# Seven block products instead of eight in three of four chunks of the MLP up projections

## The chip, the cores and the metric

The program runs on one core of a Trainium2 chip. A core has a matrix engine (TensorE, PE in the profile), which multiplies a stationary 128x128 block with a moving operand and adds into one of eight PSUM banks; three engines for elementwise work (VectorE or DVE, ScalarE or ACT, GpSimd or POOL); and a queue (SyncE or SP) that issues most of the transfers from memory. Each engine works through its own instructions in order, and engines wait for one another through semaphores. The metric is the time of one execution on the device, in microseconds (us).

## The reference

Two layers of a decoder trunk, with 528 tokens (16 learned ones ahead of 512), 1024 features wide, all in float32. The part that matters here is the MLP at the end of each layer:

```python
a = rmsnorm(h, mlp_pre_g[l])
f = jnp.square(jax.nn.relu(a @ w_up[l])) @ w_down[l]      # 1024 -> 4096 -> 1024
h = h + rmsnorm(f, mlp_post_g[l])
```

Ahead of it each layer has a mixer: an input projection, sliding-window attention with sinks beside a short gated convolution, and an output projection. The output drops the 16 learned tokens, so layer 1's MLP works on 512 tokens only.

## The kernel before

**Layout.** Features lie on the 128 partitions, tokens along the free axis. `h`, `z`, `a` and `f` are arrays of 8 feature blocks of 128 x 528. A product with a weight matrix goes by weight tiles: one tile gives 128 output features and has 8 blocks (k) of 128x128, one for each block of input features.

**Precision.** Each float32 operand is held as two parts, hi (rounded by a copy on ACT) and lo (the remainder, a subtraction on DVE). `mm3` makes one product of blocks out of three matmuls, hi x hi, hi x lo and lo x hi (L157, L158, L159). All three add into the same PSUM bank.

**Tokens.** In layer 0 a weight tile meets the tokens in two ranges, 272 and 256 columns (`RA`, `RB`). In layer 1's MLP it meets all 512 at once (`full`). A matmul's moving operand is one such range.

**The MLP.** The 4096 inner features go in 4 chunks (`NCH`) of 1024. For each chunk `mlp` makes 8 up tiles (a to f, evacuated by `f_evac`: relu on DVE out of PSUM, square on ACT, split into hi on ACT and lo on DVE) and then 8 down tiles (f to z, `z_evac`: a copy in the first chunk, later an addition on DVE). The norm's scale isn't applied to `a` but later; so `a` is h times a gain. In chunk 1 the first 5 up tiles are made together with the norm at the end of the mixer.

**Weights.** The list `blocks` holds all weight tiles of the program in order of use. `prep` loads the next one (512 KB, issued by SP, into one of two buffers `wraw`), and `cast` splits it in two halves of 128x512 (L98 on ACT, L99 on DVE). `tile_done`, called when a tile's products are written down, lets `refill` prepare as many more as keep 7 tiles ready (`CAP`; 5 in the mixer, `PCAP`).

**Order.** A scheduler that knows the dependences fixes each engine's order of instructions when the program is built; it may move an instruction ahead of others of its engine. The waits themselves are then what the chip makes of it.

Of the kernel before, what the change touches and what calls it, by code (L numbers as in the profile page):

```python
# [13 lines left out]
P = 128  # L14
# [3 lines left out]
L = 528  # L18
# [8 lines left out]
BOTH = ()  # L27
# [10 lines left out]
def trunk_kernel(ctx, tc, xT, gains, sinkb, sinkm, rope, masks, maskm, ident_in, w_in, w_out, w_up, w_down, outT):  # L38
# [57 lines left out]
    def cast(i, raw, hi, lo, pool):
        ks = slice(4 * i, 4 * i + 4)
        ACT.activation(hi[:, ks, :], raw[:, ks, :], AF.Copy)  # L98
        (POOL if i in pool else DVE).tensor_tensor(lo[:, ks, :], raw[:, ks, :], hi[:, ks, :].bitcast(F32), ALU.subtract)  # L99

    def prep(pool=(), beside=None):

        if len(prepared) == len(blocks):
            return
        kind, l, sub = blocks[len(prepared)]
        raw = wp.tile([P, KT, P], F32, tag="wraw", name="wraw", bufs=2)
        hi = wp.tile([P, KT, P], F32R, tag="w", name="whi", bufs=2 * CAP)
        lo = wp.tile([P, KT, P], F32R, tag="w", name="wlo", bufs=2 * CAP)
        dma = nc.sync.dma_start
        if beside:  # L110

            for i in range(2):
                ks = slice(4 * i, 4 * i + 4)
                dma(raw[:, ks, :], w_in[l].rearrange("(k p) m -> p k m", p=P)[:, ks, sub:sub + P])
                beside[2 * i]()
                cast(i, raw, hi, lo, pool)
                beside[2 * i + 1]()
            prepared.append((hi, lo))
            return
        if kind == "in":  # L120
            last_load[:] = [dma(raw, w_in[l].rearrange("(k p) m -> p k m", p=P)[:, :, sub:sub + P])]
        elif kind == "out":
            col = slice(P * sub, P * sub + P)
            for g in range(2):
                dma(raw[g * 64:(g + 1) * 64, 0:4, :],
                    w_out[l, g * 256:(g + 1) * 256, col].rearrange("(j p) m -> p j m", p=64))
            dma(raw[:, 4:8, :], w_out[l, 512:1024, col].rearrange("(k p) m -> p k m", p=P))
        elif kind == "up":
            dma(raw, w_up[l].rearrange("(k p) m -> p k m", p=P)[:, :, P * sub:P * sub + P])
# [22 lines left out]
    def tile_done(pool=(), most=9):  # L152
        done[0] += 1
        refill(pool, most)

    def mm3(ps, whi, wlo, ahi, alo, first, last):
        PE.matmul(ps, whi, ahi, start=first, stop=False)  # L157
        PE.matmul(ps, whi, alo, start=False, stop=False)  # L158
        PE.matmul(ps, wlo, ahi, start=False, stop=last)  # L159
# [222 lines left out]
    def first_tiles(act, pB, rA, rB, nxt):  # L382
# [602 lines left out]
```

## Time and profile before

| | us |
|---|---|
| median of 3 runs | 1174.88 (1174.23 to 1175.05) |
| the profiled execution | 1173.51 |
| its span in the trace | 1171.4 |
| PE busy, of the span | 1122.2 |
| DVE busy | 683.1 |
| ACT busy | 550.8 |
| one chunk of layer 0's MLP (up, then down) | 46.88 + 46.88 |
| one chunk of layer 1's MLP (up, then down) | 44.60 + 44.60 |

The span is what the trace covers; the time has some 2 us more around it. In the rows that follow L157 is line 157 of the kernel, and `ps<-a_hi,whi` says what is written and what is read. A group's line gives its count, then busy time in us and the mean duration of one in ns, then how long its engine had been idle before it and what ended that. A line of waits gives the sum in us, how often, and the longest. A line of the timeline gives start, length, engine, line, operation, tiles and shape, and in brackets the idle time ahead of it. Matmuls are pipelined: one starts long before the one ahead of it has ended.

### The profile page before, as it was taken

Reading aid. Unit: us, or ns where it says so; the run is one execution under the profiler, and the core shown is the slowest. Engines: PE = TensorE matmul, PEld = TensorE weight load, DVE = VectorE, ACT = ScalarE, POOL = GpSimd, SP = SyncE. Lnnn points to the kernel's source line nnn. Section 1 sums busy time; section 2 is a strip of 40 time slices with the busy share of each in tenths; the row PEclk is TensorE's granted clock in tenths of the full one; section 3 lists DMA queues with packets and bytes.
Section 4 is the critical chain, followed back from the end, with each engine's and each line's share of the span. In section 5 each row is a group of like instructions: output and inputs, shape, how many; then the busy total and the mean of one; then the engine's idle time right before and its main releaser. Section 6 shows DMA issues by size and latency. Waiting matters only on the chain. (4 is left out here: it accounts for less than half of the span.)

```text
span 1171.4 us, 19765 instructions
## 1 busy us (share of the span) xinstructions
PE 1122.2 (96%) x7778; PEld 1050.6 (90%) x7778; DVE 683.1 (58%) x1613; ACT 550.8 (47%) x1286; POOL 19.0 (2%) x54
## 2 busy tenths in 40 slices
PE   8999899899999999999989997998999999999995
PEld 7999899899999999999979997898888888888895
DVE  7988877762353354355589778777623433433435
ACT  7565776563342242244366557665523412422432
POOL 3000000000000000000000000000000000000001
PEclk9999999899999999999989999998999999999998
DMA  7242122243333333333131321222433333333302
GB/s 229 65 127 73 50 60 84 61 133 88 95 91 87 94 90 89 94 91 90 34 103 50 110 73 36 73 76 70 135 99 90 91 101 97 90 91 104 93 1 72
DMA packets 195069, 101.92 MB, mean 87 GB/s; under 512 B 4832, under 2 KB 194928, under 8 KB 194976
## 3 DMA queue, kind: packets, MB, share of 16 engines
q1 hardware_dynamic: 194368, 100.14, 29.7%
q8 instruction: 61, 1.00, 0.4%
q10 hardware_dynamic: 432, 0.32, 0.1%
q14 instruction: 32, 0.26, 0.1%
q0 software_dynamic: 176, 0.21, 0.1%
HBM read 97.88 MB, written 2.10 MB: 85 GB/s over the span
## 5 line engine op out<-in xcount | busy, mean ns | idle before, releaser
L157 PE MATMUL ps<-a_hi,whi 128*128 128x256 f32 (+3 forms) x1384 | 426.5, 309 | 6.8 <-ACT a_hi L294 5.8
L158 PE MATMUL ps<-a_lo,whi 128*128 128x256 f32 (+3 forms) x1384 | 423.2, 306 | 4.9 <-DVE a_lo L299 4.2
L159 PE MATMUL ps<-a_hi,wlo 128*128 128x256 f32 (+3 forms) x1384 | 421.5, 305 | 0.1
L98 ACT ACTIVATE whi<-wraw 128x512 fp32r<-128x512 f32 x360 | 207.1, 623 | 368.9 <-PE ps L158 337.4
L157 PE MATMUL ps<-f_hi,whi 128*128 128x256 f32 (+2 forms) x1072 | 326.4, 306 | 0.0
L158 PE MATMUL ps<-f_lo,whi 128*128 128x256 f32 (+2 forms) x1072 | 326.1, 305 | 0.0
L159 PE MATMUL ps<-f_hi,wlo 128*128 128x256 f32 (+2 forms) x1072 | 325.2, 305 | 0.0
L99 DVE TENSOR_TENSOR wlo<-wraw,whi 128x512 fp32r<-128x512 f32 x360 | 233.9, 687 | 106.4 <-ACT whi L98 100.1
L157 PEld LDWEIGHTS ps<-a_hi,whi 128*128 128x128 f32 x1384 | 265.6, 192 | 19.9 <-ACT a_hi L294 7.7
L158 PEld LDWEIGHTS ps<-a_lo,whi 128*128 128x128 f32 x1384 | 265.7, 192 | 18.2 <-DVE a_lo L299 6.6
L159 PEld LDWEIGHTS ps<-a_hi,wlo 128*128 128x128 f32 x1384 | 266.5, 193 | 10.1 <-DVE wlo L99 0.4
L158 PEld LDWEIGHTS ps<-f_lo,whi 128*128 128x128 f32 x1072 | 201.4, 188 | 9.8
L159 PEld LDWEIGHTS ps<-f_hi,wlo 128*128 128x128 f32 x1072 | 201.8, 189 | 9.1
L157 PEld LDWEIGHTS ps<-f_hi,whi 128*128 128x128 f32 x1072 | 200.9, 188 | 9.7
L469 DVE TENSOR_TENSOR z<-z,ps 128x272 f32<-128x272 f32 (+2 forms) x78 | 38.1, 488 | 148.0 <-PE ps L159 148.0
L241 DVE TENSOR_TENSOR acc<-acc,t 128x256 f32<-128x256 f32 (+1 forms) x133 | 56.4, 425 | 17.2 <-ACT t L240 15.3
L868 DVE TENSOR_SCALAR t<-ps 128x272 f32<-128x272 f32 (+1 forms) x74 | 31.5, 430 | 54.9 <-PE ps L159 54.8
L868 DVE TENSOR_SCALAR u<-ps 128x512 f32<-128x512 f32 x27 | 18.7, 692 | 69.8 <-PE ps L159 69.8
L869 ACT ACTIVATE t<-t 128x272 f32<-128x272 f32 (+1 forms) x74 | 30.4, 415 | 46.3 <-DVE t L868 46.3
L245 DVE TENSOR_TENSOR f_lo<-t,f_hi 128x272 fp32r<-128x272 f32 (+1 forms) x74 | 31.5, 432 | 25.8 <-ACT f_hi L244 25.8
L240 ACT ACTIVATE t<-z 128x256 f32<-128x256 f32 (+1 forms) x55 | 22.0, 414 | 51.3 <-DVE z L469 37.5
L294 ACT ACTIVATE a_hi<-h,gt 128x256 fp32r<-128x256 f32 (+1 forms) x48 | 24.4, 509 | 26.9 <-DVE h L288 26.7
(130 smaller groups left out, 839.6 us busy)
## 6 DMA issues: line engine op xcount, KB each, us to landing
wraw<-in_w_up SPq DMA_DIRECT2D x64, 512.0 KB
wraw<-in_w_down SPq DMA_DIRECT2D x64, 512.0 KB
wraw<-in_w_in SPq DMA_DIRECT2D x34, 512.0 KB
wraw<-in_w_out SPq DMA_DIRECT2D x32, 128.0 KB
wraw<-in_w_out SPq DMA_DIRECT2D x16, 256.0 KB
outT<-h SPq DMA_DIRECT2D x14, 128.0 KB
h<-in_xT SPq DMA_DIRECT2D x4, 272.0 KB
wraw<-in_w_in SPq DMA_DIRECT2D x4, 256.0 KB
```

What stands on the lines that cost most here:

```text
L98: ACT.activation(hi[:, ks, :], raw[:, ks, :], AF.Copy)
L99: (POOL if i in pool else DVE).tensor_tensor(lo[:, ks, :], raw[:, ks, :], hi[:, ks, :].bitcast(F32), ALU.subtract)
L157: PE.matmul(ps, whi, ahi, start=first, stop=False)
L158: PE.matmul(ps, whi, alo, start=False, stop=False)
L159: PE.matmul(ps, wlo, ahi, start=False, stop=last)
L240: ACT.activation(sq, src, AF.Square)
L241: return (eng or DVE).tensor_tensor(acc, acc, sq, ALU.add)
L245: DVE.tensor_tensor(lo, src, hi.bitcast(F32), ALU.subtract)
L294: self.act = ACT.activation(a_hi[:, k, t0:t1], hk, AF.Copy, scale=g)
L469: DVE.tensor_tensor(zz, zz, ps, ALU.add)
L868: DVE.tensor_scalar(f, ps, 0.0, None, ALU.max)
L869: ACT.activation(f, f, AF.Square)
```

## The change

In chunks 2, 3 and 4 of both layers' up projections, two weight tiles (outputs m and m+1) are taken together with two halves of the tokens (264 and 264 in layer 0, 256 and 256 in layer 1: N0 and N1) and two halves of the input features (k 0 to 3 and 4 to 7). That makes a product of 2x2 blocks with 2x2 blocks, which is done in Winograd's form of Strassen's scheme: seven block products of 4 k each instead of eight.

- *Weights.* A11 and A12 are tile m's two feature halves, A21 and A22 those of tile m+1. `prep_pair` loads the four halves and makes S1 = A21 + A22, S2 = A11 - S1, S3 = A21 - A11 and S4 = A12 + S2, four additions of 128x512 on DVE. All seven left operands are split into hi and lo: seven casts a pair, where two tiles took four.
- *Activations.* B11, B21 are the feature halves over N0, B12, B22 over N1. `fast_sums` makes T1 = B12 - B11 (which overwrites B12 in `a`), T2 = T1 - B22, T3 = B12 - B22 and T4 = B21 + T2, once per layer, after the first four down tiles of chunk 1. They lie in the attention's key and value arrays and in a new array `tx`; `clear_pad` zeroes the keys' padding again ahead of layer 1.
- *Products.* `fast_pair` runs A11 B11 (bank b1), S2 T2 (b6), S3 T3 (b7), S1 T1 (b5), and then adds A12 B21 onto b1, A22 T4 onto b7 and S4 B22 onto b5, each after the bank has been read. Six reads of PSUM on DVE and one on ACT combine them into the four blocks of f; relu, square and split follow.
- *Bookkeeping.* All weights are now loaded in halves of 256 KB, into five half buffers. Prefetch is counted in halves: a product of the new kind counts one, a normal tile two, and 14 are kept ready. The scratch space for transfers issued by software is cut to 1024 bytes.

The core of the diff:

```diff
+    def half():
+        return wp.tile([P, 4, P], F32, tag="wraw", name="wraw", bufs=5)
+    def cast(raw, hi, lo):
+        ACT.activation(hi, raw, AF.Copy)
+        DVE.tensor_tensor(lo, raw, hi.bitcast(F32), ALU.subtract)
+    def prep_pair(l, m, n):
+        if n == 0:
+            for name, k, mm in (("A11", 0, m), ("A21", 0, m + 1), ("A22", 4, m + 1), ("A12", 4, m)):
+                pair[name] = half()
+                nc.sync.dma_start(pair[name], w_up[l].rearrange("(k p) m -> p k m", p=P)[:, k:k + 4, P * mm:P * mm + P])
...
+        f = wp.tile([P, KT, P], F32R, tag="w", name="wf", bufs=2 * CAP)
+        if n == 1:
+            pair["S1"], pair["S2"] = (utile()[:, :512].rearrange("p (k m) -> p k m", k=4) for _ in range(2))
+            DVE.tensor_tensor(pair["S1"], pair["A21"], pair["A22"], ALU.add)
+            DVE.tensor_tensor(pair["S2"], pair["A11"], pair["S1"], ALU.subtract)
+        if n == 2:
+            pair["S3"] = pair["A21"]
+            DVE.tensor_tensor(pair["S3"], pair["A21"], pair["A11"], ALU.subtract)
+        if n == 6:
+            pair["S4"] = pair["S2"]
+            DVE.tensor_tensor(pair["S4"], pair["A12"], pair["S2"], ALU.add)
+        cast(pair[("A11", "S2", "S3", "S1", "A12", "A22", "S4")[n]], f[:, 0:4, :], f[:, 4:8, :])
...
-        while len(prepared) - done[0] < cap[0] and len(prepared) < len(blocks) and most:
-            prep(pool)
+        while len(prepared) < len(blocks) and taken[0] + size(len(prepared)) <= 2 * cap[0] and most:
+            prep()
...
+    def fast_sums(l, k):
...
+        DVE.tensor_tensor(d, h[:, k, N1], h[:, k, N0], ALU.subtract)
+        ACT.activation(x, h[:, k + 4, N1], AF.Copy, scale=g2)
+        hi, lo = parts("T1")
+        ACT.activation(hi, d, AF.Copy, scale=g1)
+        DVE.scalar_tensor_tensor(t2, d, g1, x, ALU.mult, ALU.subtract)
+        DVE.scalar_tensor_tensor(lo, d, g1, hi.bitcast(F32), ALU.mult, ALU.subtract)
+        DVE.scalar_tensor_tensor(t3, h[:, k, N1], g1, x, ALU.mult, ALU.subtract)
+        split(*parts("T2"), t2)
+        DVE.scalar_tensor_tensor(t4, h[:, k + 4, N0], g2, t2, ALU.mult, ALU.add)
+        split(*parts("T3"), t3)
+        split(*parts("T4"), t4)
+    def fast_pair(l, m):
...
+        b1, b6, b7, b5 = (bank()[:, :n] for _ in range(4))
+        def product(ps, name, onto=False):
+            whi, wlo = prepared[wtile()]
+            hi, lo = T[name]
+            for k in range(4):
+                mm3(ps, whi[:, k, :], wlo[:, k, :], hi[:, k, :], lo[:, k, :], not onto and k == 0, k == 3, onto)
+            tile_done()
+        def plus(a, ps):
+            t = tmp(n)
+            DVE.tensor_tensor(t, a, ps, ALU.add)
+            return t
+        def out(x, m, N):
+            ACT.activation(x, x, AF.Relu)
+            ACT.activation(x, x, AF.Square)
+            split(f_hi[:, m, N], f_lo[:, m, N], x)
+        product(b1, "B11")
+        p1 = tmp(n)
+        ACT.activation(p1, b1, AF.Copy)
+        product(b6, "T2")
+        u2 = plus(p1, b6)
+        product(b7, "T3")
+        u3 = plus(u2, b7)
+        product(b5, "T1")
+        out(plus(u3, b5), m + 1, N1)
+        product(b1, "B21", True)
+        x = tmp(n)
+        DVE.tensor_scalar(x, b1, 0.0, None, ALU.max)
+        ACT.activation(x, x, AF.Square)
+        split(f_hi[:, m, N0], f_lo[:, m, N0], x)
+        product(b7, "T4", True)
+        out(plus(u2, b7), m + 1, N0)
+        product(b5, "B22", True)
+        out(plus(u2, b5), m, N1)
...
         for c in range(NCH):
-            for m in range(NA if c == 0 else 0, 8):
-                one(lambda r: f_evac(m, r), act_a)
+            if c == 0:
+                for m in range(NA, 8):
+                    one(lambda r: f_evac(m, r), act_a)
+            else:
+                for m in range(0, 8, 2):
+                    fast_pair(l, m)
             last = c == NCH - 1
             if last:
                 new_acc("h")
             for m in range(2 if last else 8):
                 one(lambda r: z_evac(m, r, c > 0, last, (l, G_MPOST)), act_f)
+                if c == 0 and m < 4:
+                    fast_sums(l, m)
```

The scheduler places the new instructions, so the diff doesn't show their order. On VectorE, at the start of an up projection of layer 0, evacuations (relu out of PSUM, L868, and the low part, L245) and casts (L99) followed each other like this before:

```order
L868 TENSOR_SCALAR t<-ps 128x272
L245 TENSOR_TENSOR f_lo<-t,f_hi 128x272
L868 TENSOR_SCALAR t<-ps 128x256
L99 TENSOR_TENSOR wlo<-wraw,whi 128x512 x2
L245 TENSOR_TENSOR f_lo<-t,f_hi 128x256
```

Now the first pair of chunk 3 begins as follows. L955 is an addition out of PSUM, L974 the maximum with zero out of PSUM, L281 the low part of f, L109 a weight cast, and L131, L124 are the weight sums S4 and S1.

```order
L955 TENSOR_TENSOR t<-t,ps 128x264
L109 TENSOR_TENSOR wf<-u,wf 128x512
L955 TENSOR_TENSOR t<-t,ps 128x264
L131 TENSOR_TENSOR u<-wraw,u 128x512
L109 TENSOR_TENSOR wf<-wraw,wf 128x512
L955 TENSOR_TENSOR t<-t,ps 128x264
L109 TENSOR_TENSOR wf<-u,wf 128x512
L974 TENSOR_SCALAR t<-ps 128x264
L109 TENSOR_TENSOR wf<-wraw,wf 128x512
L124 TENSOR_TENSOR u<-wraw 128x512
L281 TENSOR_TENSOR f_lo<-t,f_hi 128x264
L955 TENSOR_TENSOR t<-t,ps 128x264
```

Casts and sums of later weights now stand between the reads of PSUM that free a bank, up to three between two of them.

On TensorE, where an up projection of layer 0 ends and the down projection begins, the rows before were these, the last matmuls on `a` and then the first on `f`:

```order
L158 MATMUL ps<-a_lo,whi 128x256
L159 MATMUL ps<-a_hi,wlo 128x256
L157 MATMUL ps<-f_hi,whi 128x272
L158 MATMUL ps<-f_lo,whi 128x272
L159 MATMUL ps<-f_hi,wlo 128x272
```

Now (L193 to L195 are `mm3`) the first six matmuls of the down projection, its k 0 and 1, stand ahead of the pair's last two products, A22 T4 and S4 B22; here the end of A12 B21 and the first of the six:

```order
L194 MATMUL ps<-a_lo,wf 128x264
L195 MATMUL ps<-a_hi,wf 128x264
L193 MATMUL ps<-f_hi,whi 128x272
L194 MATMUL ps<-f_lo,whi 128x272
L195 MATMUL ps<-f_hi,wlo 128x272
```

After the last product follow, in layer 0, 12 matmuls of 272 and 18 of 256 columns and then 18 of a second tile, before the first that reads feature blocks 6 and 7 of f; in layer 1, 12 matmuls of 512 columns.

More of the change, by code (lines that the diff above doesn't have):

```diff
@@ L26 @@
 LAST_ON_POOL = (3, 6)
-BOTH = ()
 EPS = 1e-6
@@ L94, in trunk_kernel @@
     used = [0]
[L96 to L101, printed above, removed]
+    done = [0]
+    taken = [0]
+    cap = [CAP]
+    def half():
[3 more added lines that the diff above has]
+        DVE.tensor_tensor(lo, raw, hi.bitcast(F32), ALU.subtract)
@@ L103, in prep @@
+    def prep(beside=None):
         if len(prepared) == len(blocks):
             return
+        taken[0] += size(len(prepared))
         kind, l, sub = blocks[len(prepared)]
-        raw = wp.tile([P, KT, P], F32, tag="wraw", name="wraw", bufs=2)
+        if kind == "upx":
+            return prep_pair(l, *sub)
         hi = wp.tile([P, KT, P], F32R, tag="w", name="whi", bufs=2 * CAP)
         lo = wp.tile([P, KT, P], F32R, tag="w", name="wlo", bufs=2 * CAP)
-        dma = nc.sync.dma_start
-        if beside:
+        raws = []
+        for i in range(2):
+            raw = half()
+            raws.append(raw)
+            ks = slice(4 * i, 4 * i + 4)
+            dma = nc.sync.dma_start
+            if kind == "out":
+                col = slice(P * sub, P * sub + P)
+                if i == 0:
+                    for g in range(2):
+                        dma(raw[g * 64:(g + 1) * 64], w_out[l, g * 256:(g + 1) * 256, col].rearrange("(j p) m -> p j m", p=64))
+                else:
+                    dma(raw, w_out[l, 512:1024, col].rearrange("(k p) m -> p k m", p=P))
+            elif kind == "down":
+                c, m = sub
+                dma(raw, w_down[l, c * 1024:(c + 1) * 1024, P * m:P * m + P].rearrange("(k p) m -> p k m", p=P)[:, ks, :])
+            else:
+                src, off = (w_in, sub) if kind == "in" else (w_up, P * sub)
+                last_load[:] = [dma(raw, src[l].rearrange("(k p) m -> p k m", p=P)[:, ks, off:off + P])]
+            if beside:
+                beside[2 * i]()
+                cast(raw, hi[:, ks, :], lo[:, ks, :])
+                beside[2 * i + 1]()
+        if not beside:
@@ L133, in prep @@
-        for i in range(2):
-            cast(i, raw, hi, lo, pool)
+                cast(raws[i], hi[:, ks, :], lo[:, ks, :])
         prepared.append((hi, lo))
@@ new lines, in fast_sums @@
+    def fast_sums(l, k):
+        N0, N1, T = fast(l)
+        n = N0.stop - N0.start
+        g1, g2 = (gt[:, l, G_MPRE + i:G_MPRE + i + 1] for i in (k, k + 4))
+        d, x, t2, t3, t4 = (tmp(n) for _ in range(5))
+        parts = lambda name: [t[:, k, :] for t in T[name]]
+        DVE.tensor_tensor(d, h[:, k, N1], h[:, k, N0], ALU.subtract)
[9 more added lines that the diff above has]
+        split(*parts("T4"), t4)
```

82 lines of the change are left out of this document (43 added, 39 removed).

## The prediction

> **What bounds the kernel now.** I read the page's first table, then busy time by stage, then single rows. The first says that TensorE (PE) is the engine to look at:
>
> ```profile
> span 1171.4 us, 19765 instructions
> PE 1122.2 (96%) x7778; PEld 1050.6 (90%) x7778; DVE 683.1 (58%) x1613; ACT 550.8 (47%) x1286; POOL 19.0 (2%) x54
> ```
>
> A mean over the span says nothing on the stages that change, so next come the stretches (length; busy time of PE, weight loads, VectorE, ScalarE, GpSimd; clock; DMA share; GB/s). The first two lines are the up and the down projection of chunk 2 in layer 0, the next two those of chunk 2 in layer 1:
>
> ```profile
> 306.15:353.03 46.88, 46.88 (x387) 46.88 (x385) 23.27 (x46) 21.49 (x47) 0.00 (x0) 1.00 0.31 91
> 353.03:399.91 46.88, 46.88 (x387) 46.88 (x385) 17.64 (x33) 9.94 (x18) 0.00 (x0) 1.00 0.32 91
> 889.40:934.00 44.60, 44.60 (x193) 36.05 (x192) 19.40 (x31) 17.81 (x32) 0.00 (x0) 1.00 0.32 95
> 934.00:978.60 44.60, 44.60 (x193) 36.06 (x192) 15.82 (x26) 10.39 (x19) 0.00 (x0) 1.00 0.33 95
> ```
>
> PE is busy in every microsecond, at a granted clock of 1.00. VectorE (DVE) and ScalarE (ACT) work half the time or less, and what they wait for is PE:
>
> ```profile
> ACT whi L98 <- PE ps L158: 337.4, 107, 5.8
> DVE z L469 <- PE ps L159: 148.0, 74, 5.3
> DVE u L868 <- PE ps L159: 69.8, 25, 3.8
> SPq L129 <- DVE wlo L99: 307.0, 56, 16.8
> ```
>
> The last line says that up-weight loads wait for a free buffer, 307 us in all: loads run ahead. So in these stages a matmul less is time less, until another engine fills up.
>
> **What a matmul costs.** Matmuls overlap, so a row's duration (about 0.29 us) is no price; the distance between the evacuations of finished tiles is. Layer 0:
>
> ```profile
> 403.12 0.44 DVE L868 TENSOR_SCALAR t<-ps 128x272 f32<-128x272 f32 x1 [1.17 <-PE ps L159]
> 405.97 0.42 DVE L868 TENSOR_SCALAR t<-ps 128x256 f32<-128x256 f32 x1 [1.00 <-PE ps L159]
> 408.98 0.44 DVE L868 TENSOR_SCALAR t<-ps 128x272 f32<-128x272 f32 x1 [0.76 <-PE ps L159]
> ```
>
> From 403.12 to 405.97 lie 24 matmuls of 256 columns: 0.1188 us each. From 403.12 to 408.98 lie 48, half of 256 and half of 272: 0.1221 on average, which is also my price for 264 columns. Layer 1, 24 matmuls of 512 between two rows, 0.2321 each:
>
> ```profile
> 894.97 0.69 DVE L868 TENSOR_SCALAR u<-ps 128x512 f32<-128x512 f32 x1 [3.85 <-PE ps L159]
> 900.54 0.69 DVE L868 TENSOR_SCALAR u<-ps 128x512 f32<-128x512 f32 x1 [2.74 <-PE ps L159]
> ```
>
> **The change on PE.** A pair of weight tiles took 2 tiles x 8 k x 3 matmuls over all tokens. Now it takes 7 products x 4 k x 3 = 84 matmuls over half of them. Per chunk of four pairs that is 336.
> - Layer 0: 46.88 becomes 336 x 0.1221 = 41.0; 5.86 less, in three chunks 17.6.
> - Layer 1: 44.60 becomes 336 x 0.1188 = 39.9; 4.7 less, in three chunks 14.1. Here one eighth (5.6) isn't reached, because two matmuls of 256 cost 0.2376 and one of 512 0.2321. In return weight loads, 81% busy in this stage now, go to what layer 0 shows, 100%; there they hold at 0.1188 a step, so I charge no more.
>
> Together 31.7 us. PE gets 1008 matmuls of 264 and 1008 of 256 columns for 1152 of 272 and 256 and 576 of 512. The order of the changed kernel shows all of them, with nothing done twice: it does what it says.
>
> **The change on DVE and ACT.** This is where it could be lost. Back-to-back prices first (the next instruction's start counts, not the duration, 0.69 for the cast):
>
> ```profile
> L99 DVE TENSOR_TENSOR wlo<-wraw,whi 128x512 fp32r<-128x512 f32 x360 | 233.9, 687 | 106.4 <-ACT whi L98 100.1 <-PE ps L158 0.2
> L98 ACT ACTIVATE whi<-wraw 128x512 fp32r<-128x512 f32 x360 | 207.1, 623 | 368.9 <-PE ps L158 337.4 <-DMA wraw<-in_w_in 15.7 <-DMA wraw<-in_w_down 11.7
> 46.27 1.29 DVE L99 TENSOR_TENSOR wlo<-wraw,whi 128x512 fp32r<-128x512 f32 x2
> 47.48 0.42 DVE L524 TENSOR_TENSOR t<-t 128x256 f32<-128x256 f32 x1
> 27.04 0.43 DVE L540 TENSOR_TENSOR u<-ps,rt 128x272 f32<-128x272 f32 x1
> 27.39 0.47 DVE L350 SCALAR_TENSOR_TENSOR a_lo<-h,gt,a_hi 128x256 fp32r<-128x256 f32 x1
> 727.66 1.14 ACT L98 ACTIVATE whi<-wraw 128x512 fp32r<-128x512 f32 x2
> 728.71 0.51 ACT L611 ACTIVATE S<-S,ng 128x256 f32<-128x256 f32 x1
> 715.14 1.61 ACT L759 ACTIVATE f_hi<-t 128x256 fp32r<-128x256 f32 x4
> ```
>
> A DVE cast or a weight sum of 512 costs 1.21 / 2 = 0.605; an addition out of PSUM 0.35, the low part of a split likewise. On ACT a cast is 0.525, an evacuation step 1.61 / 4 = 0.40.
>
> Per chunk DVE gets 24 evacuations out of PSUM, 16 low parts, 28 casts and 5 weight sums during the up stage (the order puts the other 11 into the down stage): 40 x 0.35 + 33 x 0.605 = 34 us of 41. ACT: 28 x 0.525 + 48 x 0.40 = 34 us of 41. Both rise from half busy to 83%. Uneven, though: prefetch runs 14 products ahead, so the first two pairs of a chunk prepare products (7 casts and 4 sums a pair) and the last two prepare down tiles. In the first pair of chunk 3 the order has 11 weight rows, 6 evacuations and 3 low parts: 11 x 0.605 + 9 x 0.35 = 9.8 us, against 84 x 0.1221 = 10.26 on PE. That is 96%, and 98% in layer 1 (84 x 0.1188 = 10.0). The densest stretch of the present trace with an unbroken PE is this, DVE 26.19 of 29, 90%:
>
> ```profile
> 29.00:58.00 29.00, 29.00 (x242) 28.95 (x241) 26.19 (x67) 17.82 (x47) 0.87 (x3) 1.00 0.25 66
> ```
>
> At that 90% the pair's rows take 10.9 us, 0.6 to 0.9 longer than PE. So DVE falls behind by some 1.5 us in the first two pairs and catches up in the other two. What does a delay do? Nothing else waits on DVE there but weights, which lie 14 products ahead, and PSUM banks. Eight banks hold two pairs, so a new pair takes free ones. Three products of a pair accumulate onto a bank that must have been read first: onto b1 three products after its first use, onto b7 and b5 two products after, 24 matmuls or 2.93 us. The addition needs 0.44, so about 2.5 us of lag are covered. I charge 0.4 us a chunk for single late rows, 2.4 in all; what the lag costs without that cover stands under the rivals.
>
> The handover from up to down is the other place. The last product's result runs through an addition, relu, square and a split. Today's four steps took from 309.36 to 311.20 = 1.84 us; a fifth makes 2.3:
>
> ```profile
> 309.36 0.44 DVE L868 TENSOR_SCALAR t<-ps 128x272 f32<-128x272 f32 x1 [1.17 <-PE ps L159]
> 310.76 0.44 DVE L245 TENSOR_TENSOR f_lo<-t,f_hi 128x272 fp32r<-128x272 f32 x1 [0.96 <-ACT f_hi L244]
> ```
>
> In layer 0 the order leaves 48 matmuls (5.9 us) before f's feature blocks 6 and 7 are read: covered. In layer 1 it leaves 12 of 512 columns, 2.8 us, with other rows queued ahead: I charge 0.5 us in each of three chunks, 1.5.
>
> The half sums of the activations, 32 rows on DVE and 20 on ACT, come once per layer in chunk 1's down stage, before the weights for chunk 2's first products. They cost 32 x 0.42 = 13.4 and 20 x 0.40 = 8 us, and these stages have room (DVE 11.18 of 46.85 and 11.63 of 44.60) even with 11 weight sums (6.7) on top of as many casts as now:
>
> ```profile
> 259.30:306.15 46.85, 46.85 (x387) 46.85 (x385) 11.18 (x18) 15.03 (x33) 0.00 (x0) 1.00 0.32 91
> 844.80:889.40 44.60, 44.60 (x193) 36.06 (x192) 11.63 (x18) 13.77 (x26) 0.00 (x0) 1.00 0.35 101
> ```
>
> PE's cover there is the whole down stage; uncovered, 21 us a layer.
>
> Weight loads become halves of 256 KB: the same bytes, twice the issues on SP. In the MLP SP has room. In the mixers the small rope transfers share SP's queue and may leave earlier or later; five half buffers instead of two whole ones free a little earlier. I take 0, with bounds of 2 us either way (ACT's waits for w_in loads, 15.7 above, are all there is to win). The padding memsets on GpSimd run while it is idle: 0.
>
> Sum: -31.7 + 2.4 + 1.5 = -27.8. The profiled execution took 1173.51 (span 1171.4), so 1145.7; the median is 1.4 higher, 1174.88, which gives **1147**.
>
> **A rule against it.** After idle moments close together this trace shows the clock halved:
>
> ```profile
> 206.49 0.39 PE L157 MATMUL ps<-a_hi,whi 128*128 128x272 f32 x1 [0.77 <-ACT a_hi L294]
> 208.00 0.39 PE L158 MATMUL ps<-a_lo,whi 128*128 128x272 f32 x1 [1.11 <-DVE a_lo L299]
> 211.76 1.22 PE L196 MATMUL ps<-acc,ones 128*128 128x256 f32 x2 [1.27 <-DVE acc L241]
> ...
> 213.00 0.43 PE L158 MATMUL ps<-a_lo,whi 128*128 128x272 f32 x1
> 213.23 0.43 PE L159 MATMUL ps<-a_hi,wlo 128*128 128x272 f32 x1
> ...
> 216.84 0.28 PE L157 MATMUL ps<-a_hi,whi 128*128 128x272 f32 x1
> 216.96 0.29 PE L158 MATMUL ps<-a_lo,whi 128*128 128x272 f32 x1
> ...
> 740.99 0.50 PE L163 MATMUL ps<-p,vv 128*128 128x512 f32 x1 [1.63 <-ACT p L244]
> 741.33 0.28 PE L157 MATMUL ps<-f_hi,whi 128*128 128x256 f32 x1
> 741.45 0.28 PE L158 MATMUL ps<-f_lo,whi 128*128 128x256 f32 x1
> ```
>
> From 213.00 to 216.84 stand 17 matmuls at 0.226, where 272 columns cost 0.125 at full clock (405.97 to 408.98, 24 of them): 1.7 us lost. After the single gap of 1.63 us at 740.99 steps stayed at 0.12. The Trainium skill ("TensorE: Matmul & The Clock Gate", section "A second HAM failure mode: psum-queue depth-cycling") says that a PE which cycles through PSUM banks and idles a little between groups lets its clock swing between half and full. By that rule gaps at every pair would cost 1.7 us each on top, 24 x 1.7 = 41 us more (an estimate from the row), and the change would be slower; by the row at 740.99 a lone gap every 10 us costs its own length. My sum goes by the row, and has hardly a gap.
>
> **Rivals.**
> - *Nothing is lost* (0.10): all cover holds, mixers gain a little. 31.7 off: 1143. For it: lags stay under 2.5 us by the sum. Against: 96% of DVE is more than any stretch here shows.
> - *DVE sets the pace* in the first two pairs (0.15). At full durations (0.69 and 0.44) the first pair's rows come to 11 x 0.69 + 9 x 0.44 = 11.5 us, 1.3 more than PE; 12 such pairs 15.6, with handovers of 1 us in six chunks 21.6: 31.7 - 21.6 leaves 10.1, 1165. For it: casts hand over between ACT and DVE, both over 80% busy. Against: back-to-back rows at 0.605.
> - *PE stops at the re-used bank* (0.08, slower). If the addition that reads b5 stands behind casts that wait for ACT or for a load, PE waits in front of the pair's last product, and every later product is late by as much, which nothing makes up. It decides from 31.7 / 24 = 1.32 us a pair; at 1.5 it is 36 us, 1174.9 - 31.7 + 36 = 1179. It needs a lag of 4 us, some seven weight rows. This is where the clock rule above would come in. Against: between two evacuations the order has at most three such rows.
> - Between the last two, gain and loss even out (0.05): 1175.
>
> **How the numbers follow.** The forecast, 1147, has 0.62 and its own range, 1143 to 1155: no loss at one end; at the other 1.2 us of lag in six chunks, 1 us in three handovers and 2 us in the mixers, 12.2 together. About 0.2% (2.3 us) is what a measurement here can tell from no change. Faster: 0.62 + 0.10 + 0.15 = 0.87; same 0.05; slower 0.08. The range goes from 1141 (full gain and 2 us in the mixers) to 1165, where the pace case ends; outside lie the slower case, the even one and a little of the others.
>
> **What would show it.** Right: up stages of 41.0 to 42 us (layer 0) and 39.9 to 41 (layer 1) with PE busy throughout, DVE and ACT near 34 us there; down stages unchanged; 8066 matmuls; chunk 1's down stage still 46.9 and 44.6. Wrong: idle PE ahead of matmuls on b5 or b7, released by DVE additions; rows of 0.23 us per matmul in up stages; mixers that changed by more than 2 us.

## The result and the profile after

The changed kernel takes 1140.62 us (median of 4 runs, 1140.13 to 1141.1); the kernel before takes 1174.97 (4 runs beside them). The ratio is 0.9709, 95% interval 0.9692 to 0.9726: 34.3 us less, where 27.8 were forecast. The time lies 0.4 us below the lower end of the predicted range. Two later measurements of the same changed kernel gave 0.972 (0.9707 to 0.9733) and 0.9713 (0.9697 to 0.9729), 33.4 and 34.2 us.

The first table of the page after:

```profile
span 1138.8 us, 21453 instructions
PE 1088.9 (96%) x8066; PEld 1042.9 (92%) x8066; DVE 822.3 (72%) x1941; ACT 641.2 (56%) x1542; POOL 20.2 (2%) x56
```

PE's busy time falls by 33.3 us, the span by 32.6; DVE's rises by 139. The stretches of the kernel after (length; busy time of PE, weight loads, DVE, ACT, GpSimd; clock; DMA share; GB/s): chunk 1's down stage and chunk 2's up and down stages in layer 0, then the same three in layer 1.

```profile
258.82:305.59 46.77, 46.77 (x386) 46.77 (x385) 29.31 (x60) 22.02 (x53) 0.00 (x0) 1.00 0.22 63
305.59:347.24 41.65, 41.65 (x345) 41.65 (x343) 34.03 (x70) 31.90 (x73) 0.00 (x0) 1.00 0.45 130
347.24:393.27 46.03, 46.03 (x381) 46.03 (x379) 24.64 (x45) 10.74 (x21) 0.00 (x0) 1.00 0.23 67
...
826.42:871.01 44.59, 44.59 (x193) 36.07 (x192) 21.86 (x37) 14.97 (x28) 0.00 (x0) 1.00 0.23 65
871.01:912.17 41.16, 41.16 (x344) 40.89 (x342) 34.11 (x71) 32.03 (x74) 0.00 (x0) 1.00 0.47 135
912.17:955.53 43.36, 43.36 (x188) 35.03 (x187) 22.00 (x36) 10.41 (x20) 0.00 (x0) 1.00 0.24 68
```

PE is busy in every microsecond of them. Each up stage here holds six matmuls of the down projection that the scheduler drew forward, so the comparable number is a whole chunk: 41.65 + 46.03 = 87.68 in layer 0 against 93.76 before, 41.16 + 43.36 = 84.52 in layer 1 against 89.20. That is 6.08 and 4.68 us a chunk, three times each: 32.3 of the 32.6 by which the span shrank. Chunk 1's down stage, with the half sums of the activations in it, is unchanged (46.77, 44.59). The rest of the program gives 0.3 in all: the stretch to chunk 2 is 0.56 shorter, layer 1 up to its chunk 2 is 0.62 longer (301.94 after, 301.32 before), and 0.4 lies behind the six chunks. The stretch from layer 1's start to its chunk 2, before:

```profile
587.87:889.19 301.32, 281.20 (x1941) 261.69 (x1940) 214.18 (x566) 171.75 (x432) 2.49 (x10) 0.95 0.29 82
```

And after:

```profile
569.07:871.01 301.94, 280.50 (x1941) 261.44 (x1940) 231.61 (x608) 178.06 (x451) 2.48 (x10) 0.95 0.27 77
```

Does DVE fall behind, as forecast? Yes. The timeline of the kernel after in chunk 2's first pair, three rows of PE and then four of DVE:

```profile
311.31 0.28 PE L195 MATMUL ps<-a_hi,wf 128*128 128x264 f32 x1
...
314.25 0.28 PE L195 MATMUL ps<-tx,wf 128*128 128x264 f32 x1
314.37 0.29 PE L193 MATMUL ps<-a_hi,wf 128*128 128x264 f32 x1
...
312.33 0.42 DVE L955 TENSOR_TENSOR t<-t,ps 128x264 f32<-128x264 f32 x1
...
314.81 0.69 DVE L124 TENSOR_TENSOR u<-wraw 128x512 f32<-128x512 f32 x1 [1.11 <-DMA wraw<-in_w_up]
315.41 0.69 DVE L109 TENSOR_TENSOR wf<-wraw,wf 128x512 fp32r<-128x512 f32 x1
316.02 0.42 DVE L955 TENSOR_TENSOR t<-t,ps 128x264 f32<-128x264 f32 x1
```

S1 T1 ends on b5 at about 311.6; it is read at 312.33, 0.7 us late. The next product on b5 starts at 314.37, 1.6 us after that read is done. A22 T4 ends at 314.5 and is read at 316.02, 1.5 us late, behind a weight sum, which had waited 1.11 us for its load, and a cast. Nothing on PE waits for either. Over all 24 pairs the reads that free b7 and b5 are at most 1.4 us late.

### The profile page after: what moved, and what is told of

Its sections match the earlier page's. It is cut to its first block, busy times and chain, and to the rows that moved or that the text cites. A ratio compares the mean times of both kernels' runs of the same rounds, so it can differ in the third digit from the quotient of the medians.

```text
span 1138.8 us, 21453 instructions
## 1 busy us (share of the span) xinstructions
PE 1088.9 (96%) x8066; PEld 1042.9 (92%) x8066; DVE 822.3 (72%) x1941; ACT 641.2 (56%) x1542; POOL 20.2 (2%) x56
## 4 chain that ended last, share of the span: by engine, by line
PE 87%; DVE 7%; ACT 3%; issue 1%; DMA 1%; SPq 0%; DVEq 0%; POOL 0%; ACTq 0%
PE ps L195 28%; PE ps L193 28%; PE ps L194 27%; PE ps L199 2%; DVE wlo L109 1%; PE ps L232 1%; ACT S L647 1%; DMA h<-in_xT 1%; DVE acc L277 1%; PE ps L693 1%; DVE p L281 1%; DVE a_lo L335 0%; DVE S L658 0%; DVE z L706 0%; DVE h L324 0%
## 5 line engine op out<-in xcount | busy, mean ns | idle before, releaser
L195 PE MATMUL ps<-f_hi,wlo 128*128 128x256 f32 (+2 forms) x1072 | 325.4, 305 | 0.0
L193 PE MATMUL ps<-f_hi,whi 128*128 128x256 f32 (+2 forms) x1072 | 323.7, 306 | 0.0
L193 PE MATMUL ps<-a_hi,whi 128*128 128x256 f32 (+3 forms) x808 | 242.5, 302 | 7.2 <-ACT a_hi L330 6.2
L194 PE MATMUL ps<-a_lo,whi 128*128 128x256 f32 (+3 forms) x808 | 238.5, 295 | 4.6 <-DVE a_lo L335 4.1
L195 PE MATMUL ps<-a_hi,wlo 128*128 128x256 f32 (+3 forms) x808 | 237.1, 294 | 0.3 <-DVE wlo L109 0.3
L195 PEld LDWEIGHTS ps<-f_hi,wlo 128*128 128x128 f32 x1072 | 201.9, 189 | 9.2
L193 PEld LDWEIGHTS ps<-f_hi,whi 128*128 128x128 f32 x1072 | 200.1, 188 | 9.3
L109 DVE TENSOR_TENSOR wlo<-wraw,whi 128x512 fp32r<-128x512 f32 x264 | 173.1, 686 | 44.0 <-ACT whi L108 21.3
L193 PEld LDWEIGHTS ps<-a_hi,whi 128*128 128x128 f32 x808 | 157.7, 196 | 11.9 <-ACT a_hi L330 8.2
L194 PEld LDWEIGHTS ps<-a_lo,whi 128*128 128x128 f32 x808 | 158.2, 196 | 9.3 <-DVE a_lo L335 6.5
L195 PEld LDWEIGHTS ps<-a_hi,wlo 128*128 128x128 f32 x808 | 158.5, 196 | 1.8 <-DVE wlo L109 0.5
L194 PE MATMUL ps<-a_lo,wf 128*128 128x264 f32 (+1 forms) x384 | 108.0, 283 | 0.0
L193 PE MATMUL ps<-a_hi,wf 128*128 128x264 f32 (+1 forms) x384 | 107.8, 283 | 0.0
L195 PE MATMUL ps<-a_hi,wf 128*128 128x264 f32 (+1 forms) x384 | 107.1, 283 | 0.0
L109 DVE TENSOR_TENSOR wf<-wraw,wf 128x512 fp32r<-128x512 f32 x96 | 65.5, 686 | 10.9 <-ACT wf L108 9.8
L194 PEld LDWEIGHTS ps<-a_lo,wf 128*128 128x128 f32 x384 | 72.2, 188 | 0.1
```

Source lines behind the costliest of these rows:

```text
L109: DVE.tensor_tensor(lo, raw, hi.bitcast(F32), ALU.subtract)
L193: PE.matmul(ps, whi, ahi, start=first, stop=False, skip_group_check=onto)
L194: PE.matmul(ps, whi, alo, start=False, stop=False, skip_group_check=onto)
L195: PE.matmul(ps, wlo, ahi, start=False, stop=last, skip_group_check=onto)
```

## The experiments

The kernel before was run again beside each group: 1173.26 us beside the first four kernels, 1173.56 beside the two lighter loads, the scratch and the first repeat, 1174.07 beside x_cover2, the heavier loads and the two edits together, 1173.35 and 1174.36 beside the buffer runs. Ratios are to these.

**Bookkeeping alone** (x_halves): loads in halves, five half buffers, the new counting of prefetch; every up projection as before.

```diff
-            if c:
+            if False:
                 blocks += [("upx", l, (8 * c + 2 * m, n)) for m in range(4) for n in range(7)]
...
-            if c == 0:
-                for m in range(NA, 8):
+            if True:
+                for m in range(NA if c == 0 else 0, 8):
...
-                if c == 0 and m < 4:
-                    fast_sums(l, m)
```

> All up projections as before; only the bookkeeping of the change stays (weights loaded in halves of 256 KB into five buffers, prefetch counted in halves, smaller scratch space). Theory (the gain is matmuls alone): 1175, within 1.5 of before. Rival (loads in halves speed up the start or the mixers, and that is the gain beyond the forecast): 1172 or less.

1170.44 us, ratio 0.9978 (0.9966 to 0.9989): 2.6 us less, just outside the bound of 2 that the prediction had set, so the rival of this run holds.

**The seven products in layer 0 alone** (x_layer0).

```diff
-            if c:
+            if c and l == 0:
                 blocks += [("upx", l, (8 * c + 2 * m, n)) for m in range(4) for n in range(7)]
...
-            if c == 0:
-                for m in range(NA, 8):
+            if c == 0 or l != 0:
+                for m in range(NA if c == 0 else 0, 8):
...
-                if c == 0 and m < 4:
+                if c == 0 and m < 4 and l == 0:
```

> Seven products in layer 0 only. Theory: three chunks of 6.1 us as the trace of the changed kernel shows, so 1175 - 18.2 = 1156.8, and layer 1 is the rest, 14 to 16. Rival (the two layers help each other, for example through the mixer between them): more than 2 us away from that.

1155.61 us, ratio 0.9848 (0.9825 to 0.9871). Chunk 2 of layer 0, up and down stage, in x_halves:

```profile
307.03:353.80 46.77, 46.77 (x386) 46.77 (x385) 23.27 (x46) 21.50 (x47) 0.00 (x0) 1.00 0.31 91
353.80:400.58 46.78, 46.78 (x387) 46.78 (x385) 17.62 (x33) 9.96 (x18) 0.00 (x0) 1.00 0.32 91
```

The same in x_layer0:

```profile
307.67:349.31 41.64, 41.64 (x344) 41.64 (x343) 34.10 (x70) 31.95 (x73) 0.00 (x0) 1.00 0.45 131
349.31:395.34 46.03, 46.03 (x380) 46.03 (x379) 24.64 (x45) 10.74 (x21) 0.00 (x0) 1.00 0.23 66
```

With the bookkeeping the same on both sides the seven products take 93.55 to 87.67, 5.88 us a chunk; the prediction's step has 5.86.

**How much cover the re-used banks need** (x_cover2, x_cover1, x_cover0): the seven products held to one order, with two, one or no product between the use of b7 and b5 and their re-use. The first is the control: the change's own order, but fixed.

```diff
+            with ExitStack() as es:
+                if last_mm:
+                    es.enter_context(tc.issue_after(last_mm[0].ins))
+                for k in range(4):
...
         product(b5, "T1")
         out(plus(u3, b5), m + 1, N1)
-        product(b1, "B21", True)
...
         product(b7, "T4", True)
         out(plus(u2, b7), m + 1, N0)
         product(b5, "B22", True)
         out(plus(u2, b5), m, N1)
+        product(b1, "B21", True)
...
```

That is x_cover1 (x_cover2 has the first hunk alone: each product's matmuls are issued after those of the product ahead). x_cover0 also runs T4 ahead of T1, so that T4 follows T3 on b7, and B22 follows T1 on b5.

> The changed kernel with the seven products of a pair held to one order, B11 T2 T3 T1 B21 T4 B22 (two products between the use of b7 or b5 and its re-use), which is the control for the two fixed orders with less between. If the loss of the order with one product between comes from the re-used banks, this one takes 1140 to 1141. If it comes from holding the order at all, which keeps TensorE from taking other matmuls in between, it takes 1142 to 1143 as well.

> The products of a pair stand in a fixed order with one product (1.46 us) instead of two between the first use of banks b7 and b5 and their re-use. Theory (VectorE reads banks 0.7 to 2.2 us late, and two products of cover hide it): TensorE waits up to 1 us at a re-use in the first two pairs of a chunk, 1146 to 1156. Rival (VectorE is never late, cover isn't needed): 1141 to 1143. Rival (gaps at each pair halve the clock): above 1165.

> The same with nothing between: T4's product follows T3's on b7, B22's follows T1's on b5. Theory: each of 48 re-uses waits for the end of the last matmul and the read, at least 0.8 us, and for VectorE's lag in half of them, some 1 us: 1179 to 1203, slower than before. Rival (never late): 48 x 0.8 = 38, 1179. Rival (the clock falls to half after such gaps): 48 x 1.7 more, above 1250, with matmul steps of 0.23 us.

x_cover2 takes 1140.87 us, ratio 0.972 (0.9706 to 0.9735), as the free order. x_cover1 takes 1142.52, 0.9735 (0.9712 to 0.9757), below the 1146 to 1156 expected; in its trace the chunks are 0.6 to 0.9 us longer, some 4 us in all six, and the rest of the program is shorter. x_cover2 has no such loss, so it isn't the held order. x_cover0 takes 1182.24, 1.0074 (1.0051 to 1.0098): **slower than before**. Its chunks are 7.3 to 8.7 (layer 0) and 6.6 to 7.5 us (layer 1) longer, 46 us in all for 48 re-uses, some 3 of them by half clock at the end of two stages. Two of PE's rows in x_cover0's first pair and two stretches of it, chunk 2's up stage in each layer (with 35 and 27 matmuls of the down projection drawn into them):

```profile
310.38 0.39 PE L195 MATMUL ps<-tx,wf 128*128 128x264 f32 x1 [0.52 <-DVE t L963]
...
314.10 0.39 PE L195 MATMUL ps<-a_hi,wf 128*128 128x264 f32 x1 [0.52 <-DVE t L963]
...
305.31:359.22 53.91, 48.52 (x374) 47.03 (x373) 35.52 (x71) 33.11 (x75) 0.00 (x0) 0.97 0.35 103
...
891.60:944.36 52.76, 47.87 (x364) 45.26 (x363) 35.18 (x71) 32.94 (x75) 0.00 (x0) 1.00 0.36 105
```

PE stands idle ahead of seven of the eight re-uses of an up stage until an addition has read the bank: the rival "PE stops at the re-used bank", made to happen.

**More work for DVE** (x_load4, x_load7, x_load11, x_load14): so many more additions of 128x512 a pair, 0.605 us each, whose results are overwritten by the cast that follows. x_load7:

```diff
+        src = pair[("A11", "S2", "S3", "S1", "A12", "A22", "S4")[n]]
+        if n in (0, 1, 2, 3, 4, 5, 6):
+            DVE.tensor_tensor(f[:, 4:8, :], src, src, ALU.add)
-        cast(pair[("A11", "S2", "S3", "S1", "A12", "A22", "S4")[n]], f[:, 0:4, :], f[:, 4:8, :])
+        cast(src, f[:, 0:4, :], f[:, 4:8, :])
```

> Four more additions of 128x512 a pair on VectorE, in the weight preparation (16 a chunk, 0.605 us each). In the first two pairs of a chunk the changed kernel shows VectorE busy 18.1 of 20.8 us; with 8 of the additions, 4.8 us, it needs 23. Theory (VectorE is near its limit there and two products of cover take up about 2.5 us): 0.5 to 2.2 us a chunk, 1143 to 1154. Rival (VectorE has room beyond what its busy time shows): 1141.

> Seven more additions a pair, one with each product (28 a chunk). The first two pairs then need 26.6 us of VectorE for 20.8 of TensorE, the last two 15.9 as before. Theory: TensorE waits 3.5 to 5.8 us a chunk in the first two pairs, 1161 to 1176, so that most of the gain goes. Rival (the lag is caught up behind the 14 prepared products): under 1150.

> Eleven additions of 128x512 more per pair on VectorE (4 x 11 x 0.605 = 26.6 us a chunk). Theory A, the limit is VectorE's sum over the whole chunk (up and down stage), because weights are prepared 14 products ahead and the down stage makes up for the up stage: 58.7 + 26.6 = 85.3 of 87.7 us in layer 0 and 56.1 + 26.6 = 82.7 of 84.5 in layer 1, so that nothing or little is lost: 1140 to 1150. Theory B, the limit is the up stage alone (34 + 26.6 = 61 of 41 us, nothing of it moved): 20 us lost in each of six chunks, about 1260.

> Fourteen additions of 128x512 more per pair on VectorE (4 x 14 x 0.605 = 33.9 us a chunk). Theory A (VectorE's sum over the whole chunk is the limit): 58.7 + 33.9 = 92.6 of 87.7 us in layer 0 and 56.1 + 33.9 = 90.0 of 84.5 in layer 1, 4.9 and 5.5 us over in three chunks each, 31 us in all, less what the stages ahead prepared before: 1160 to 1175. Theory B (the up stage alone): 68 of 41 us, about 1300. If it takes 1140 again, VectorE isn't what can set the pace at all.

x_load4 takes 1140.27 us (0.9717, 0.9702 to 0.9732) and x_load7 1140.31 (0.972, 0.9707 to 0.9733): nothing. x_load11 takes 1160.74 (0.9905, 0.9878 to 0.9932) and x_load14 1190.12 (1.0136, 1.0119 to 1.0153): 20 and 50 us more than the change. Theory B was far off (1260, 1300); theory A had the direction, but the upper ends of its ranges were passed by 11 and 15 us. The theories of the two lighter loads had put x_load7 at 1161 to 1176; their rivals (room to spare, the lag is caught up) were right in time. The first 31 us of chunk 2 in x_load7, then its whole up stage, then the rest of the chunk:

```profile
306.27:337.30 31.03, 31.03 (x257) 31.03 (x256) 30.95 (x61) 20.57 (x46) 0.00 (x0) 1.00 0.27 78
306.27:354.87 48.60, 48.60 (x401) 48.60 (x400) 43.27 (x87) 32.71 (x75) 0.00 (x0) 1.00 0.40 115
354.87:393.94 39.07, 39.07 (x323) 39.07 (x322) 29.90 (x56) 9.85 (x19) 0.00 (x0) 1.00 0.26 75
```

DVE works without a break for 31 us and PE loses nothing. But the order isn't that of the change any more: with the additions the scheduler has made another, which draws 63 matmuls of the down projection into this up stage (25 in x_load4, 6 in the change) and moves products on re-used banks back. In chunk 2's second pair S3 T3 on b7 ends at about 321.0 and DVE reads it at 324.56, 3.5 us late, more than two products cover:

```profile
320.75 0.28 PE L198 MATMUL ps<-vv,wf 128*128 128x264 f32 x1
...
328.78 0.28 PE L196 MATMUL ps<-tx,wf 128*128 128x264 f32 x1
...
324.56 0.42 DVE L958 TENSOR_TENSOR t<-t,ps 128x264 f32<-128x264 f32 x1
```

PE comes back to b7 only at 328.78, after three products of the next pair. So the load is free because other matmuls fill the time, and not because two products are always cover enough.

Chunk 2's up stage in x_load11, with 39 matmuls of the down projection drawn into it:

```profile
305.22:354.22 49.00, 46.17 (x377) 45.75 (x376) 47.58 (x94) 31.71 (x72) 0.00 (x0) 1.00 0.38 110
```

The same in x_load14, with 55 of them:

```profile
306.20:358.83 52.63, 50.21 (x393) 49.06 (x392) 51.37 (x101) 30.55 (x72) 0.00 (x0) 0.97 0.29 83
```

And x_load14's waits of PE (us in all, how often, the longest), for weights and for a bank to be read:

```profile
PE ps L198 <- DVE wf L109: 21.1, 10, 3.6
PE ps L196 <- DVE t L958: 7.8, 7, 1.6
```

Why is the limit between 7 and 11? Weights are prepared two pairs ahead, so an up stage prepares only two of its four pairs (the other two were prepared in the down stage ahead). In the change it has 34.03 us of DVE work in 41.65: 7.6 free, which is 7.6 / 2 / 0.605 = 6.3 additions a pair, and more where matmuls of the down projection make the stage longer. With 11 a pair it is 34.0 + 22 x 0.605 = 47.3, with 14 it is 50.9: the measured 47.58 and 51.37, in stages that are now DVE's (97 and 98% busy). This sum was made after the runs, not before; it gives DVE's load, but not why the scheduler makes room for 7 additions and not for 11.

**Both together** (x_cover1_load7): one product of cover in a held order and seven additions a pair, each of which costs little or nothing alone (the edits are those of x_cover1 and of x_load7).

> One product between use and re-use of b7 and b5 (order B11 T2 T3 T1 T4 B22 B21), and seven additions of 128x512 more per pair on VectorE. Theory: the planner's rows out of PSUM stand at most two or three weight rows behind a product's end (0.9 to 2.4 us late), and two products (2.93 us) hide this even with VectorE unbroken; with one product (1.46 us) and a full VectorE, reads 1.0 to 2.0 us late meet a cover of 1.46 - 0.44 = 1.0 us, so that up to 1 us is lost at some of the 48 re-uses: 1150 to 1180. Rival: reads go ahead of weight rows whenever they are ready, so that the load delays weights alone: 1142 to 1144, as without the load.

1181.33 us, ratio 1.0065 (1.0049 to 1.0081): 41 us more than the change, just above the range expected, and slower than before. PE and then DVE in chunk 3's second pair:

```profile
414.11 0.29 PE L200 MATMUL ps<-vv,wf 128*128 128x264 f32 x1
...
418.28 0.39 PE L198 MATMUL ps<-tx,wf 128*128 128x264 f32 x1 [2.43 <-DVE t L966]
...
415.31 0.68 DVE L128 TENSOR_TENSOR wraw<-wraw 128x512 f32<-128x512 f32 x1
...
417.21 0.68 DVE L109 TENSOR_TENSOR wf<-wraw,wf 128x512 fp32r<-128x512 f32 x1
417.81 0.42 DVE L966 TENSOR_TENSOR t<-t,ps 128x264 f32<-128x264 f32 x1
```

S3 T3 on b7 ends at about 414.4 and is read at 417.81, 3.4 us late, behind five rows of other work (415.31 to 417.81). So on a full DVE reads do fall behind by whole queues of other rows, as the first theory had it. In x_load7 a read was as late (3.5 us), and there the scheduler was free to put other products in between; here the held order forbids it. Two products of cover would leave 2.5 us for a lag, less than 3.4, so this run doesn't tell whether one product less or the held order did it: the held order of x_cover2 with the load wasn't run.

**Which part of the bookkeeping** (x_scratch, x_halves5, x_halves4, x_halves6): the kernel before with only the scratch space cut; then x_halves again with five half buffers, with four (as many bytes as the two whole ones of before) and with six.

```diff
-    nc = _bacc.Bacc("TRN2", target_bir_lowering=False, num_devices=1)
+    nc = _bacc.Bacc("TRN2", target_bir_lowering=False, num_devices=1, dynamic_dma_scratch_size=1024)
```

That is x_scratch; this x_halves4:

```diff
-        return wp.tile([P, 4, P], F32, tag="wraw", name="wraw", bufs=5)
+        return wp.tile([P, 4, P], F32, tag="wraw", name="wraw", bufs=4)
```

> The kernel before with only the scratch space for software transfers cut to 1024 bytes. Loads in halves and the rest of the bookkeeping gave 2.6 us without a product saved. If the loads in halves are the cause: no change, 0 +- 1 us. If it is where the arrays lie or the scratch itself: 2 to 3 us faster.

> Half loads into five half buffers with every up projection as before, in more rounds. Both theories below take this one at 1169.5 to 1172; at 1173.5 or more the 2.6 us measured of it were run-to-run spread, and the products alone gained all.

> The same with four half buffers, which hold as many bytes as the two whole ones of the kernel before. If the fifth buffer brings the 2.6 us, this takes 1173 to 1174. If the halves bring them, because a weight's first half can be cast when half of it has come and a buffer comes free after one cast instead of two, it takes 1170 to 1171.5.

> Half loads into six half buffers, every up projection as before. If the 3.5 us that six buffers brought to the changed kernel lie in layer 1's mixer alone, and don't need the seven products, this takes 1167 to 1168; if they lie with the pairs' four loads at a time, it stays at 1170.9.

x_scratch takes 1173.67 us (1.0, 0.999 to 1.0009): nothing. x_halves5 takes 1170.91 (0.9977, 0.9967 to 0.9987), x_halves4 1170.94 (0.9977, 0.9965 to 0.999), x_halves6 1172.0 (0.9984, 0.9973 to 0.9994). So the gain of 2 to 2.6 us is real, and it isn't the number of buffers or the scratch space. The loads in halves are left as the likely cause; the new array `tx` and the zeroing of the padding are in all four x_halves kernels too and weren't taken out, and prefetch counted in halves is the same as before where all tiles count two.

**More buffers in the changed kernel** (x_bufs6, x_bufs7), with the change itself measured again (after_again, unchanged, and after_third, unchanged, beside x_bufs7). x_bufs6:

```diff
-        return wp.tile([P, 4, P], F32, tag="wraw", name="wraw", bufs=5)
+        return wp.tile([P, 4, P], F32, tag="wraw", name="wraw", bufs=6)
```

> The changed kernel with six half buffers instead of five. If the number of buffers brings something, another 0.5 to 2 us, 1138 to 1140; if only the halves do, 1140 to 1141.

> The changed kernel with seven half buffers. If each further buffer lets the loads run further ahead at the layer's start, 1134 to 1136; if six already cover it, 1136.5 to 1137.5.

> The changed kernel again, beside the others on the same chip, to tell its gain from that of the bookkeeping alone (0.9978 of before, 2.6 us). If the two add up: 0.971, 34 us, of which 31.6 are the matmuls. If the first measurement was a lucky one: 0.973 to 0.976.

> The changed kernel itself, beside the kernels with six and seven half buffers: 1140 to 1141 by every theory.

x_bufs6 takes 1136.69 us (0.9686, 0.9671 to 0.97; 1138 to 1140 was expected at best), x_bufs7 1134.49 (0.9664, 0.9645 to 0.9683), the change 1140.19 and 1140.2: **six or seven buffers beat the change by 3.5 to 5.7 us**; six and seven aren't told apart (1135.27 to 1137.79 against 1132.32 to 1136.59). The gain isn't in the stages of the change (a chunk takes 87.6 and 84.5 us with six as with five). It lies in layer 1's mixer. Its length in after_again up to the output projection and PE's wait for the norm at its end:

```profile
570.58:723.22 152.64, 136.16 (x1038) 130.94 (x1037) 127.82 (x375) 94.51 (x253) 2.47 (x10) 0.93 0.25 72
...
714.95 1.22 PE L232 MATMUL ps<-acc,ones 128*128 128x256 f32 x2 [7.62 <-DVE acc L277]
```

The same of x_bufs6, with one more wait:

```profile
569.77:718.77 149.00, 135.61 (x1039) 130.28 (x1038) 128.28 (x377) 95.99 (x256) 2.47 (x10) 0.94 0.26 73
...
706.52 0.76 PE L693 MATMUL ps<-ident,S 128*128 128x128 f32 x5 [2.17 <-DVE S L653]
710.12 1.22 PE L232 MATMUL ps<-acc,ones 128*128 128x256 f32 x2 [2.46 <-DVE acc L277]
```

The kernel before has waits of 1.47 and 2.46 us there, in a stretch as long as that of the change:

```profile
587.87:741.33 153.46, 138.50 (x1038) 132.51 (x1037) 128.62 (x377) 96.74 (x256) 2.49 (x10) 0.93 0.25 71
...
729.08 1.13 PE L657 MATMUL ps<-ident,S 128*128 128x128 f32 x8 [1.47 <-DVE S L617]
...
732.67 1.22 PE L196 MATMUL ps<-acc,ones 128*128 128x256 f32 x2 [2.46 <-DVE acc L241]
```

So the change waits 3.7 us longer at this place (7.62 against 3.93) and less at others, and the sixth buffer takes 3 of the 3.7 out again (2.17 + 2.46). The products don't bring the wait: x_halves6 has none of them and has it too (7.61). DVE's rows show what differs. In after_again the maximum of a softmax (`ng`, L643) stands behind two weight casts and two other splits:

```profile
708.96 1.29 DVE L109 TENSOR_TENSOR wlo<-wraw,whi 128x512 fp32r<-128x512 f32 x2
...
710.58 1.28 DVE L281 TENSOR_TENSOR p<-ps,p 128x512 fp32r<-128x512 f32 x2
711.77 0.16 DVE L643 TENSOR_SCALAR ng<-mx 128x4 f32<-128x4 f32 x1
```

In x_bufs6 it stands ahead of the casts:

```profile
705.94 0.17 DVE L643 TENSOR_SCALAR ng<-mx 128x4 f32<-128x4 f32 x1
...
707.48 1.28 DVE L109 TENSOR_TENSOR wlo<-wraw,whi 128x512 fp32r<-128x512 f32 x2
```

So the number of buffers acts through the order that the scheduler makes of it; that this one row is the cause was read from the rows and not tested alone. It is no rule that more buffers help: x_halves6 has the long wait, and x_halves with five has two shorter ones (2.13 and 4.04).

## Why the prediction was right, and where it wasn't

**The change on PE: right.** 5.86 a chunk in layer 0 and 4.7 in layer 1 were forecast; with equal bookkeeping (x_halves against the change) the traces have 93.54 to 87.67 and 89.16 to 84.52, 5.87 and 4.64. In sum 31.5 for the 31.7 forecast. The weight loads, 99% busy in layer 1's up stage, cost nothing more, as assumed.

**The charges of 2.4 and 1.5 us: wrong, both are nothing.** This is the step that failed. The 2.4 were for "single late rows" of DVE, the 1.5 for the handover from up to down in layer 1. PE has no idle time in any of these stages. The step mixed up a late reader with a late PE: it had worked out itself that 2.5 us of lag are covered, and the reads that free b7 and b5 are at most 1.4 us late. x_cover1 and x_cover0 give the price that the charge should have been weighed against: about 4 us in all with one product of cover, 46 with none. At the handover it had counted 2.8 us of matmuls for a chain of 2.3 us and charged for rows queued ahead of it all the same; PE didn't wait there either.

**The bookkeeping at 0: too little.** Alone it gives 2 to 2.6 us, at the edge of its bounds. In the change some 0.8 of that stands in the six chunks (a chunk of layer 0 takes 93.76 us before and 93.55 in x_halves); the rest of the program, where the prediction had looked for it, gives 0.3.

**The account.** From the profiled execution before (1173.51) to that after (1140.60) are 32.9 us: 31.5 by the products, 0.8 by the bookkeeping in the chunks, 0.3 in the rest of the span and 0.3 around it. The forecast of 1145.7 for it had 31.7 and 3.9 in charges. The 1.4 us that were then added because the profiled execution before lay below its median didn't come back: the one after lies on its median. 3.9 + 1.2 + 1.4 = 6.5, the whole miss. The lower end of the range, 1141, had the charges at nothing already; that the time lies 0.4 below even this comes from the bookkeeping and that 1.4. The 0.4 itself is less than the spread of the medians of the kernel before (1173.26 to 1174.97).

**DVE and ACT at 34 of 41 us: right** (34.03 and 31.90 in layer 0, 34.11 and 32.03 in layer 1). But 96% of DVE in the first pair of chunk 3 didn't come: it is 7.97 of 10.26 us there (78%), with waits for loads and casts, and 10.27 of 10.27 in the second pair. It was also the wrong window to worry about. A stage's last two pairs even it out, and x_load7 shows DVE full for 31 us at no cost, in an order made for it.

**The rivals.** *Nothing is lost* was the case, and had been given only 0.10. *DVE sets the pace* isn't this kernel's case, but is real from between 7 and 11 more additions a pair on. *PE stops at the re-used bank* needs less cover (x_cover0), or less cover, a held order and a full DVE (x_cover1_load7); both then end slower than before, so its mechanism and its sign were right. Its break-even of 1.32 us a pair fits: x_load11 loses 20 us (0.84 a pair) and stays faster than before, x_cover0 loses 42 (1.7 a pair) and is slower.

**The clock rule** was to add 1.7 us for each gap. In x_cover0 two gaps of 0.5 to 0.7 us a pair leave the steps behind them at 0.12 us, so by the trace it doesn't come with gaps of that size. The Trainium skill ("TensorE: Matmul & The Clock Gate", section "A second HAM failure mode: psum-queue depth-cycling") has the clock swing where PE idles a little between groups of matmuls; these gaps didn't make it swing. Longer ones do, and then a lone gap is enough, so the row at 740.99 was no rule either; the last section shows what decides.

## What to carry to other kernels

Before charging for a late engine, ask what its lateness holds up, and compare the lag with the work between a buffer's use and its re-use: here two products (2.9 us) made a lag of up to 1.4 us free, one cost some 4 us, none 46. Take an engine's load over the stretch that the prefetch can even out, not over its densest piece. Before calling an added load free, look whether the scheduler has made another order for it. And when a change alters how weights are buffered, look for new waits far from it, since the order of everything is made anew: the last 3.5 us lay in the next layer's mixer.

## What the runs showed of the hardware

**Two changes that each cost little can cost much together.** Seven additions cost 0, one product of cover in a held order less than 2 (4 in the chunks themselves), both at once 41. Which part of the second matters beside the load wasn't told apart.

**When PE's clock falls.** x_cover1_load7 has nine gaps of 2.4 to 2.8 us in its up stages, some 13 us or more apart from each other. After five of them the clock was at half, for 14 to 26 matmuls, after four it stayed full (such as the gap at 418.28 above). The next gap in that stage, with half clock behind it:

```profile
431.33 0.59 PE L198 MATMUL ps<-tx,wf 128*128 128x264 f32 x1 [2.59 <-DVE t L966]
431.71 0.42 PE L199 MATMUL ps<-tx,wf 128*128 128x264 f32 x1
431.93 0.42 PE L200 MATMUL ps<-tx,wf 128*128 128x264 f32 x1
```

Steps of 0.22 us from 431.71 to 437.43, 26 of them, where 0.12 is the full clock: 2.6 us lost on top of the gap. What decides is not the length alone. In all traces here the stretches at half clock begin on marks 3.41 us apart and, but for one at the program's end, last one to three such steps. Two steps between such marks around the gap at 418.28, and two around that at 431.33:

```profile
413.61:417.03 3.42, 2.24 (x19) 2.03 (x17) 3.42 (x8) 0.39 (x2) 0.00 (x0) 1.00 0.44 131
417.03:420.44 3.41, 2.16 (x17) 2.16 (x18) 3.41 (x8) 1.52 (x3) 0.00 (x0) 1.00 0.07 20
...
427.27:430.68 3.41, 1.47 (x13) 1.26 (x11) 3.41 (x8) 2.02 (x6) 0.00 (x0) 1.00 0.40 118
430.68:434.10 3.42, 2.77 (x12) 2.77 (x13) 2.14 (x5) 0.42 (x1) 0.00 (x0) 0.50 0.77 220
```

The first gap is shared out over two steps, 1.2 us of idle PE in each, and the clock stays. The second puts 1.9 us into one step, and the next step has half the clock. So it is with all nine: the five have 1.9 to 2.7 us of idle PE in one step, the four at most 1.8. In x_cover0 the six gaps of 0.5 to 0.7 us that a layer-0 up stage has never add up to that; the seventh, 1.78 us at the stage's end, halved the clock where it lay in one step (two of three stages) and not where 0.1 us of it fell into the next. So in these stages the limit lies near 1.8 us of idle PE, about half of a step. It was read from the traces afterwards; no run was made for it.
